# One weight gradient by Strassen-Winograd: five plain pairs first, three resident sums, D folded into C and 7, eight additions on GpSimd

## The chip, the cores and the metric

The kernel runs on one core of one Trainium2 chip. The metric is the device time of one execution in microseconds (us); three runs of the kernel before gave 162.25, 162.35 and 162.43, median 162.35. One more execution was profiled; the lines of the profile come from that one.

## What is computed

```python
def setup_inputs():
    batch, m, k, n = 16, 512, 1024, 768
    ...
def reference(input, grad_output):            # (16, 512, 1024) and (16, 512, 768), float32
    grad_weight = np.einsum('bmk,bmn->kn', input, grad_output)
    return grad_weight.astype(np.float32)     # (1024, 768)
```

It is one matrix product: the 8192 rows of `input` (1024 columns, X in the kernel) against the 8192 rows of `grad_output` (768 columns, G), summed over the rows. The kernel rounds both to bf16 on the way in and sums in f32.

## The kernel before, in words

**Tiles.** The rows are read in 32 pairs of 256. A pair has an x tile and a g tile, bf16, loaded by DMAs that POOL issues and that convert from f32 (lines 152 and 153; up to `PAIRS_HELD` = 14 pairs are held). Only the very first pieces come as f32 over two other queues (`xf`, `gf`) and are rounded by VectorE and ScalarE (`round_by`).

**Four quarters.** The output is cut in four quarters: A (first 512 of k, left 384 of n), B (first, right), C (second, left), D (second, right). Each quarter has four blocks, q = 0 to 3, of 128 x 384, and a block fits in one of the eight PSUM banks.

**Two ways to add a pair.** `LOADS` says how each pair is multiplied. A plain pair ("s") is two steps of 128 rows, each 16 matmuls (four quarters, four blocks): 32 a pair. A Strassen pair ("P") takes seven products instead of eight: 28 matmuls of 128x384. Its products go to seven sums, each with four blocks: 1 and A (from x and g as they are), B and C (one operand raw, one a sum) and 5, 6 and 7 (both operands sums). The sums of x and of g are made on VectorE in six steps, `x0 x1 x2` (`sum_x`, lines 183 to 187) and `g0 g1 g2` (`sum_g`, lines 193 to 197). At the end the sums are combined: A + 1; 6 + 1; 7 + 6; then from 5 one gets 5 - 6 and 5 - 7; B + (5 - 6), C + 7, D + (5 - 7), where D holds the plain pairs' share alone. `SHARED` names for each sum the one that is added to it.

**32 sums, 8 banks.** There are 28 running sums of Strassen products and four of D, and eight banks. A's four blocks keep a bank each until they are complete (banks 7, 3, 4 and 1); the others take turns in banks 0, 2, 5 and 6. A block that leaves its bank is kept in SBUF (`acc` or `macc`), in one of three ways:

- `c`: ScalarE copies the bank out (`close`, line 327), for a bank that already held the whole sum;
- `v`: VectorE copies it (line 329) or adds it to what SBUF holds (line 331), and in the end adds the shared sum too (lines 307 to 312) and starts the store to DRAM, on SP's queue (ScalarE's for the last 128 columns);
- before that, `f` (`fill`, line 274) may let ScalarE copy the SBUF sum back into a bank, so that the matmuls go on adding to it.

**The order is written out by hand.** `PLAN` is one list of tokens, and each engine runs its own instructions strictly in the order of that list: `A1.2` is two matmuls on block A1, `53@6.2` opens bank 6 for block 3 of product 5 and does two matmuls, `c53`, `v53`, `f53@0` are as above, `x1.12` is a step of the sums of pair 12, `r2` a rounding. An instruction that has to wait holds up all that stands behind it on its engine. The lines: matmuls 287, fills 274, copies out 327, warm-up matmuls 135 (`WARMUP`: on constants, before the first data come).

Of the kernel before, what the change touches and what calls it, by code (L numbers as in the profile page):

```python
# [9 lines left out]
P = 128  # L10

LOADS = "ssssssPPPPPPPPPPPPPPPPPPPPPPPPPs"

PLAN = (
    "A0@7.1 A3@3.1 A1@4.1 C3@5.1 C2@0.1 C1@2.1 r0 cC3 C0@6.1 vC2 A2@1.1 cC1 D0@5.1 vC0 B0@0.1 cD0 D1@2.1 "
    "r1 r3 B3@6.1 r2 D3@5.2 vB0 r4 A1.1 A2.1 cD1 vB3 A3.1 B1@0.2 cD3 B2@2.2 vB1 D2@6.2 cB2 C0@5.1 C1@0.1 "
    "vD2 A0.1 fD0@2 A2.1 vC0 A3.1 fD1@6 A1.1 D0.2 vC1 C2@5.2 cD0 D1.2 vC2 C3@0.2 cD1 B0@2.2 vC3 B3@5.3 "
    "fB1@6 vB0 A0.2 fB2@0 vB3 B1.2 fC0@2 B2.2 cB1 C1@5.2 vB2 C0.2 fD2@6 A3.1 vC1 D3@0.2 cC0 D2.2 fC2@5 "
    "vD3 C3@2.1 A1.1 cD2 A2.1 vC3 C2.1 B0@0.1 D1@6.1 vC2 D0@2.1 vB0 fD2@5 A3.2 vD1 A1.2 fB0@0 D2.2 vD0 "
    "B1@6.2 cD2 B0.2 vB1 B2@2.2 cB0 B3@5.2 vB2 C0@6.2 fC1@0 A2.2 vB3 fC2@2 C1.2 vC0 C3@5.2 cC1 C2.2 vC3 "
    "fD0@6 A0.2 D1@0.4 vC2 D3@5.4 vD1 D0.4 vD3 C3@2.2 vD0 B3@5.2 C0@0.2 vC3 fC1@6 A3.2 vB3 fB2@2 A0.2 vC0 "
    "C1.2 fD2@5 B2.2 cC1 D2.2 vB2 C2@0.2 cD2 B0@6.2 vC2 fB1@2 A1.4 vB0 fC1@0 B1.4 C2@5.2 cB1 D2@6.2 vC2 "  # L30
    "C1.2 fD0@2 A2.4 vD2 fD3@5 vC1 fC3@6 D0.2 D3.2 vD0 C3.2 cD3 C0@0.2 vC3 B2@2.4 vC0 fB3@6 B0@5.4 vB2 "
    "fD1@0 B3.4 fC0@2 vB0 A3.1 g0.6 fB1@5 A3.3 vB3 A0.2 g1.6 A0.2 fC1@6 D1.1 g2.6 D1.3 A2.2 vD1 A1.3 x0.6 "
    "fC2@0 C0.3 C1.1 x1.6 C1.2 cC0 C2.1 x2.6 C2.2 cC1 C3@2.1 g0.7 C3.2 cC2 B1.3 fD0@6 vC3 D2@0.2 g1.7 cB1 "
    "D0.2 vD2 fD3@2 A2.1 A3.1 A0.1 g2.7 cD0 10@5.1 D3.2 c10 x0.7 11@0.2 cD3 12@6.2 v11 13@5.2 c12 50@2.1 "
    "x1.7 50.1 c13 51@0.2 x2.7 52@6.2 c50 g0.8 53@5.2 c51 70@2.2 v52 c53 A2.1 g1.8 A3.1 fB3@0 72@6.2 v70 "
    "73@5.2 c72 g2.8 B3.2 v73 63@2.2 cB3 B2@6.1 x0.8 B2.1 fC1@5 A1.2 v63 A0.2 71@0.1 x1.8 71.2 vB2 62@2.3 "
    "c71 x2.8 C1.2 c62 g0.9 60@6.3 cC1 61@2.1 g1.9 61.2 fB0@0 v60 10@5.2 c61 g2.9 B0.3 v10 fC3@6 C2@2.2 "
    "cB0 x0.9 C2.1 C3.3 fC0@5 vC2 A2.2 f52@0 C0.1 x1.9 cC3 C0.2 A3.1 x2.9 A3.1 cC0 12@2.1 g0.10 12.1 52.2 "
    "f63@5 v12 B1@6.3 c52 g1.10 63.2 f13@2 vB1 11@0.2 c63 A0.1 g2.10 13.2 v11 72@5.2 c13 x0.10 A1.2 f51@0 "
    "53@6.2 v72 A0.1 f70@2 A3.1 51.1 x1.10 f50@5 51.2 v53 70.3 c51 x2.10 50.2 f73@6 g0.11 50.1 B3@0.3 c70 "  # L40
    "v50 73.2 fB2@2 g1.11 73.1 vB3 A2.1 f10@5 B2.2 c73 g2.11 B2.1 10.1 x0.11 10.2 cB2 C1@0.3 c10 x1.11 "
    "62@6.2 f71@2 vC1 A3.1 A1.1 f61@5 A0.1 x2.11 71.2 f60@0 g0.12 71.1 61.3 v62 c71 60.1 g1.12 60.2 c61 "
    "B0@2.1 g2.12 fB1@6 B0.2 v60 11@5.2 vB0 B1.2 fC0@0 A2.1 x0.12 A2.1 cB1 A0.1 C0.3 fC2@2 v11 A3.1 fC3@6 "
    "A1.1 x1.12 C2.3 cC0 x2.12 13@5.2 f53@0 g0.13 13.1 C3.3 cC2 v13 53.2 f52@2 g1.13 53.1 vC3 12@5.3 c53 "
    "g2.13 52.3 f72@6 v12 63@0.2 x0.13 c52 63.1 72.3 f62@5 v63 A2.1 f51@2 A1.1 x1.13 62.2 c72 51.1 x2.13 "
    "51.2 f50@0 v62 73@6.3 c51 g0.14 50.3 f70@5 v73 A3.1 fB2@2 A0.1 70.1 g1.14 c50 70.2 g2.14 B3@6.3 c70 "
    "B2.1 x0.14 B2.2 10@5.3 vB3 cB2 C1@0.1 x1.14 C1.2 f60@6 v10 11@2.3 x2.14 60.2 f61@5 g0.15 60.1 A1.1 "
    "61.3 c60 vC1 A0.1 g1.15 71@6.3 c61 v11 B0@0.1 fB1@5 g2.15 B0.2 v71 A2.2 fC2@2 A3.1 x0.15 A3.1 f52@6 "
    "B1.3 vB0 C2.2 cB1 x1.15 C2.1 52.2 cC2 x2.15 52.1 C0@0.1 fC3@5 g0.16 C0.2 A1.1 c52 A0.1 vC0 C3.3 "
    "f12@2 g1.16 13@6.3 vC3 12.2 g2.16 f62@5 12.1 v13 53@0.3 c12 x0.16 62.3 f72@6 A1.1 v53 63@2.3 c62 "  # L50
    "x1.16 f50@0 72.4 v63 f51@5 50.1 g0.17 50.2 c72 70@2.1 x2.16 70.2 c50 g1.17 51.3 v70 73@6.2 g2.17 c51 "
    "73.1 B2@0.1 x0.17 fB3@2 B2.2 A2.2 fC1@5 v73 B3.3 x1.17 C1.3 vB2 cB3 10@6.2 x2.17 cC1 10.1 71@0.1 "
    "g0.18 f11@2 71.2 A3.2 v10 f60@5 11.1 g1.18 11.2 v71 60.3 c11 g2.18 61@6.3 c60 x0.18 A0.3 fC0@2 v61 "
    "B1@0.3 fB0@5 x1.18 C0.3 fC2@6 vB1 B0.2 cC0 x2.18 B0.1 C2.1 g0.19 f12@0 C2.2 C3@2.3 cB0 vC2 12.2 "
    "f62@5 g1.19 12.1 vC3 A1.2 c12 53@6.1 g2.19 53.2 f52@2 x0.19 13@0.4 v53 A3.2 52.1 x1.19 f72@6 52.3 "
    "v13 62.2 x2.19 c52 62.2 g0.20 73@0.3 c62 g1.20 63@2.4 f51@5 v73 72.1 g2.20 72.2 fC1@0 v63 51.3 c72 "
    "x0.20 A2.3 c51 70@2.1 x1.20 70.3 f71@5 x2.20 50@6.4 v70 C1.1 g0.21 C1.2 fB2@2 A0.2 v50 cC1 B2.2 "
    "g1.21 B2.2 fB3@6 g2.21 A1.2 cB2 B3.4 x0.21 71.3 cB3 B0@0.2 x1.21 c71 B0.1 10@6.2 x2.21 10.2 vB0 "
    "C2@2.2 g0.22 C2.1 f61@0 A3.2 vC2 11@5.3 g1.22 11.1 f60@2 61.4 v10 g2.22 60.4 v11 c61 x0.22 C0@6.4 "
    "f53@0 c60 12@5.1 x1.22 12.3 vC0 B1@2.2 x2.22 B1.2 g0.23 C3@6.4 v12 53.2 g1.23 53.2 vB1 A1.2 c53 vC3 "  # L60
    "52@5.3 f73@2 g2.23 13@0.2 x0.23 13.2 A2.3 v52 A0.1 x1.23 A0.2 f51@5 v13 A3.2 51.1 x2.23 51.2 g0.24 "
    "51.1 73.3 c51 g1.24 73.1 C1@6.1 g2.24 C1.2 c73 63@5.4 vC1 f72@2 70@0.1 x0.24 f71@6 70.2 72.5 v63 v70 "
    "f62@5 A1.2 x1.24 c72 71.2 g0.25 71.2 f50@0 62.1 x2.24 fB2@2 62.2 g1.25 62.2 c71 B2.1 g2.25 B2.3 c62 "
    "50.4 vB2 B0@6.1 x0.25 f10@2 B0.3 c50 C2@5.1 x1.25 C2.3 f11@0 vB0 10.2 x2.25 10.2 g0.26 11.4 c10 vC2 "
    "B3@6.2 f60@2 g1.26 B3.2 c11 g2.26 B3.1 60.4 vB3 fB1@0 61@5.2 fC0@6 x0.26 61.2 c60 B1.4 v61 12@2.1 "
    "x1.26 fC3@5 12.3 vB1 C0.2 g0.27 f53@0 C0.2 x2.26 C3.2 cC0 g1.27 C3.2 v12 53.3 cC3 g2.27 53.1 52@6.4 "
    "v53 A2.1 x0.27 f51@0 A2.3 v52 A3.3 x1.27 A3.1 f70@6 A0.2 x2.27 A0.2 g0.28 A1.3 13@2.1 g1.28 13.2 "
    "g2.28 13.1 C1@5.4 v13 51.4 f73@2 vC1 70.1 x0.28 f63@5 70.3 c51 73.1 x1.28 73.3 c70 x2.28 73.1 63.2 "
    "c73 g0.29 63.3 f72@2 50@0.1 g1.29 50.2 c63 g2.29 50.1 71@6.4 v50 f62@5 72.4 fB0@0 v71 62.1 x0.29 "
    "f11@6 62.3 c72 B0.1 x1.29 B0.3 c62 x2.29 11.4 fB2@2 vB0 fC2@5 B2.1 g0.30 B2.4 f10@0 v11 C2.4 vB2 "  # L70
    "f11@6 10.1 g1.30 f12@2 10.3 vC2 A2.1 g2.30 A2.2 c10 x0.30 12.4 f13@5 f10@0 x1.30 11.1 13.3 c12 v11 "
    "10.1 A3.1 f61@2 x2.30 A3.2 v13 f62@6 A1.3 v10 f63@5 61.5 f60@0 62.2 v61 60.5 v62 f71@2 A2.2 f72@6 "
    "v60 A3.2 A1.2 vA2 f70@0 A0.5 vA3 vA1 70.3 vA0 63.2 v70 f50@1 71.2 72.2 fC0@3 v63 50.2 f73@0 v71 C0.6 "
    "f51@4 v72 fC1@5 v50 51.3 f52@2 fC2@7 C1.5 vC0 fD0@6 v51 fB0@1 52.4 fD1@3 B0.4 vC1 fB1@4 C2.3 v52 "
    "fD2@5 B1.7 vB0 fB2@2 vC2 73.2 vB1 B2.3 v73 f53@1 D0.2 D1.2 fC3@4 vB2 53.4 vD0 C3.6 vD1 v53 fD3@0 "
    "fB3@2+7 D2.2 D3.2 vC3 B3.7 vD2 vD3 vB3 "
).split()


WARMUP = [("b", 512), ("f", 512), ("f", 512), ("b", 512)]  # L80
PAIRS_HELD = 14
SUMS_HELD = 10

MERGED = 2


@with_exitstack
def kernel(
# [162 lines left out]


    SHARED = {"A": "1", "B": "5", "C": "7", "D": "1", "6": "1", "7": "6"}

    done = {(p, q): 0 for p in streams for q in range(Q)}
    fresh = {(p, q): True for p in streams for q in range(Q)}
    closed = set()
    opened = {}
    used = {7}
    stores = [0]  # L260

    def bank(b):
        return psum.tile([P, 512], f32, name=f"bank{b}")

    def fill(p, q, b, b2):
        assert (p, q) not in opened and not fresh[p, q] and b in used
        src = sum_of(p, q)
        if b2 is None:
            parts = [(bank(b), 0, NH)]
        else:  # L270
            assert b2 in used
            parts = [(bank(b), 0, 256), (bank(b2), 256, NH)]
        for tile_, c0, c1 in parts:
            nc.scalar.copy(out=tile_[:, 0 : c1 - c0], in_=src[:, c0:c1])  # L274
        opened[p, q] = (parts, True)

    def multiply(p, q, b, n):
        first = (p, q) not in opened
        if first:
            opened[p, q] = ([(bank(b), 0, NH)], False)  # L280
            used.add(b)
        parts, carried = opened[p, q]
        for tile_, c0, c1 in parts:
            for j in range(n):
                at = done[p, q] + j
                stat, mov = operands(p, streams[p][at], q)
                nc.tensor.matmul(  # L287
                    tile_[:, 0 : c1 - c0],
                    stat,
# [7 lines left out]
    def close(engine, p, q):  # L297
# [34 lines left out]
        if final:  # L332
            closed.add((p, q))
# [51 lines left out]
```

## Time and profile before

| | |
|---|---|
| median of three runs | 162.35 us |
| the profiled execution | 162.31 us, of which the span in the profile is 160.5 us |
| granted TensorE clock, mean | 1.00 |
| loads | 58.72 MB read from DRAM |
| fills on ScalarE (line 274) | 71 + 70 instructions, some 0.48 us each |
| copies out on ScalarE (line 327) | 61 + 45 instructions, some 0.48 us each |
| adds on VectorE (line 331) | 54 + 41 instructions, some 0.55 us each |
| sums of x and g on VectorE | 25 times six instructions, 0.35 to 0.68 us each |
| instructions of POOL | DMA issues (0.53 us each) and memsets (0.10) |

How to read it. The busy table gives the time in which an engine works on at least one instruction; instructions of one engine overlap, so the distance from one start to the next in a queue that never waits (its step) is shorter than the duration that the page prints. The slices cut the span in 40 parts and give each engine's share in tenths. The chain that ended last follows the end of the span backwards, at each step to whatever released the instruction. The timeline lists merged runs: start, length, engine, line, what is written and read, and how many instructions (x4). A wait is put down to whatever came last.

### The profile page before, as it was taken

To read this page: it belongs to the slowest core of one execution; us is meant where nothing else is said; L and a number is where in the kernel's file an instruction comes from. 1 tells how busy PE (TensorE), PEld (TensorE's weight loads), DVE (VectorE), ACT (ScalarE), POOL (GpSimd) and SP (SyncE) were. 2 spreads that over 40 slices of the span, in tenths; PEclk is the share of its full clock that TensorE was granted. 3 is DMA by queue.
4 is the path that set the end of the run, shared out by engine and by line. 5 is a ranking of instruction groups with operands and counts; after the bars stand their busy time and mean duration, and the time that the engine had idled before them with its cause. 6 is when DMAs were issued, how large, how long until landed. Compare 5 with 4: busy or idle time off the path is not lost.

```text
span 160.5 us, 2776 instructions
## 1 busy us (share of the span) xinstructions
PE 155.3 (97%) x937; PEld 91.9 (57%) x937; DVE 142.7 (89%) x323; ACT 112.8 (70%) x253; POOL 34.8 (22%) x69
## 2 busy tenths in 40 slices
PE   8899999999999999999999999999999999999990
PEld 3355556556556656655655655665665665556560
DVE  0788986989999999999989998998899998989992
ACT  3779737749888999968777786534777368877730
POOL 7452222122221222222122222212222100000000
PEclk9999999999999999999999999999999999999999
DMA  5999999999999999999999999999999999924385
GB/s 176 295 213 213 210 216 213 213 213 212 213 212 212 213 213 214 210 214 213 215 214 213 213 212 212 213 212 214 213 210 213 215 212 214 212 43 157 137 294 196
DMA packets 12830, 33.40 MB, mean 208 GB/s; under 512 B 1424, under 2 KB 4624, under 8 KB 12816
## 3 DMA queue, kind: packets, MB, share of 16 engines
q0 software_dynamic: 9360, 28.64, 90.2%
q1 hardware_dynamic: 3024, 3.47, 6.3%
q10 hardware_dynamic: 432, 1.11, 1.8%
q8 instruction: 7, 0.11, 0.3%
q14 instruction: 7, 0.06, 0.1%
HBM read 58.72 MB, written 3.15 MB: 385 GB/s over the span
## 4 chain that ended last, share of the span: by engine, by line
DMA 48%; PE 44%; DVE 2%; issue 2%; POOL 1%; DVEq 0%; POOLq 0%
DMA xp<-in_input_dram 48%; PE bank L287 44%; POOL gp L157 1%; DVE acc L312 1%; DVE xe L183 0%; POOL xp L159 0%; DVE acc L331 0%; DVE macc L331 0%; DVEq L380 0%; DVE xe L185 0%; POOLq L153 0%; POOLq L369 0%; POOLq L152 0%
## 5 line engine op out<-in xcount | busy, mean ns | idle before, releaser
L287 PE MATMUL bank<-gp,xp 128*128 128x384 bf16 (+2 forms) x631 | 109.8, 324 | 0.6 <-DVE xp L201 0.6
L287 PEld LDWEIGHTS <-xp 128*128 128x128 bf16 x631 | 61.1, 98 | 42.5 <-DVE xp L201 1.3
L287 PE MATMUL bank<-ge,xe 128*128 128x384 bf16 x300 | 56.2, 326 | 0.1
L274 ACT COPY bank<-macc 128x384 f32<-128x384 f32 x71 | 33.6, 484 | 13.2 <-DVE macc L331 5.6
L287 PEld LDWEIGHTS <-xe 128*128 128x128 bf16 x300 | 29.3, 98 | 19.9 <-issue 0.6
L274 ACT COPY bank<-acc 128x384 f32<-128x384 f32 (+1 forms) x70 | 32.3, 479 | 9.1 <-DVE acc L329 5.5
L327 ACT COPY macc<-bank 128x384 f32<-128x384 f32 x61 | 28.6, 479 | 9.5 <-PE bank L287 8.1
L331 DVE TENSOR_TENSOR acc<-bank,acc 128x384 f32<-128x384 f32 x54 | 28.7, 552 | 2.8 <-PE bank L287 1.2
L153 POOL DMA_DIRECT2D xp<-in_input_dram x30 | 16.0, 532 | 53.3 <-DMA xp<-in_input_dram 28.0
L327 ACT COPY acc<-bank 128x384 f32<-128x384 f32 x45 | 21.4, 480 | 6.5 <-PE bank L287 6.0
L152 POOL DMA_DIRECT2D gp<-in_grad_output_dram x30 | 16.0, 533 | 37.1 <-DMA gp<-in_grad_output_dram 15.0
L331 DVE TENSOR_TENSOR macc<-bank,macc 128x384 f32<-128x384 f32 x41 | 22.5, 551 | 0.5 <-PE bank L287 0.2
L183 DVE TENSOR_TENSOR xe<-xp 128x1024 bf16<-128x1024 bf16 x25 | 17.1, 683 | 1.2 <-DMA xp<-in_input_dram 1.2
L329 DVE COPY acc<-bank 128x384 f32<-128x384 f32 x24 | 13.1, 553 | 3.0 <-PE bank L287 2.4
L193 DVE TENSOR_TENSOR ge<-gp 128x768 bf16<-128x768 bf16 x25 | 13.8, 550 | 0.0
L187 DVE TENSOR_TENSOR xp<-xp,xe 128x512 bf16<-128x512 bf16 x25 | 10.5, 419 | 0.4
L185 DVE TENSOR_TENSOR xe<-xe,xp 128x512 bf16<-128x512 bf16 x25 | 10.5, 418 | 0.3
L197 DVE TENSOR_TENSOR gp<-ge,gp 128x384 bf16<-128x384 bf16 x25 | 8.8, 352 | 0.3
L195 DVE TENSOR_TENSOR ge<-gp,ge 128x384 bf16<-128x384 bf16 x25 | 8.7, 350 | 0.2
L312 DVE TENSOR_TENSOR acc<-bank,macc 128x384 f32<-128x384 f32 (+2 forms) x17 | 8.0, 522 | 0.0
L329 DVE COPY macc<-bank 128x384 f32<-128x384 f32 x14 | 7.6, 552 | 0.4 <-PE bank L287 0.4
L201 DVE CAST gp<-gf 128x192 bf16<-128x192 f32 (+1 forms) x2 | 0.7, 360 | 4.9 <-DMA gf<-in_grad_output_dram 4.9
(17 smaller groups left out, 21.6 us busy)
## 6 DMA issues: line engine op xcount, KB each, us to landing
xp<-in_input_dram POOLq DMA_DIRECT2D x30, 512.0 KB, 16.9
gp<-in_grad_output_dram POOLq DMA_DIRECT2D x30, 384.0 KB, 16.7
out_dram<-acc SPq DMA_DIRECT2D x12, 192.0 KB, 1.9
xf<-in_input_dram ACTq DMA_DIRECT2D x2, 512.0 KB, 5.0
gp<-in_grad_output_dram POOLq DMA_DIRECT2D x3, 192.0 KB, 6.6
out_dram<-acc SPq DMA_DIRECT2D x6, 96.0 KB, 1.7
xp<-in_input_dram POOLq DMA_DIRECT2D x2, 256.0 KB, 8.0
gf<-in_grad_output_dram SPq DMA_DIRECT2D x2, 192.0 KB, 4.2
```

What stands on the lines that cost most here:

```text
L152: nc.gpsimd.dma_start(out=gp, in_=G[rows, :].rearrange("(p m) n -> p m n", m=2))
L153: nc.gpsimd.dma_start(out=xp, in_=X[rows, :].rearrange("(p m) k -> p m k", m=2))
L183: nc.vector.tensor_sub(out=xe[:, 0:2, :], in0=x[:, 1::-1, :], in1=x[:, 3::-2, :])
L185: nc.vector.tensor_sub(out=xe[:, 2, :], in0=xe[:, 0, :], in1=x[:, 0, :])
L187: nc.vector.tensor_add(out=x[:, 1, :], in0=x[:, 2, :], in1=xe[:, 2, :])
L193: nc.vector.tensor_add(out=ge[:, 0:2, :], in0=g[:, 0:2, :], in1=g[:, 1::2, :])
L274: nc.scalar.copy(out=tile_[:, 0 : c1 - c0], in_=src[:, c0:c1])
L287: nc.tensor.matmul(tile_[:, 0 : c1 - c0], stat, mov[:, c0:c1], start=first and j == 0, stop=True, skip_group_check=True,)
L312: nc.vector.tensor_add(out=dst[:, c0:c1], in0=b, in1=sum_of(SHARED[p], q)[:, c0:c1])
L327: nc.scalar.copy(out=dst, in_=b)
L329: nc.vector.tensor_copy(out=dst, in_=b)
L331: nc.vector.tensor_add(out=dst, in0=b, in1=dst)
```

## The change

- **Loads.** `LOADS` has five plain pairs and then 27 Strassen pairs; before, six plain ones, 25 Strassen ones and a plain one at the end.
- **Banks.** A0, A1 and A2 keep a whole bank each (`@R`: banks 5, 6 and 7) until they are complete; A3 takes turns with all the others in banks 0 to 4. Groups in a bank become shorter.
- **D.** When D's plain share is complete, it is added to C and subtracted from 7 at an eviction that these blocks have anyway (`k`, on VectorE: 8 of them). D's own result is then 5 - 7, made in the step that closes 5, and D has no late fill and eviction any more.
- **GpSimd.** Eight additions of sums in SBUF go to POOL (`add_shared`): for A0 to A3, C0 and C3 it adds the shared sum after ScalarE has copied the bank out and then stores (`q`); for blocks 60 and 72 it adds the shared sum ahead of the last eviction (`p`).
- **Warm-up.** One bf16 matmul of 512 columns and 32 of 128 instead of two f32 and two bf16 ones of 512.
- **Stores.** The first four stores are halved instead of the first three.
- **Order.** `PLAN` is new from its first token to its last. Its beginning and its end are shown.

```diff
-LOADS = "ssssssPPPPPPPPPPPPPPPPPPPPPPPPPs"
+LOADS = "sssssPPPPPPPPPPPPPPPPPPPPPPPPPPP"
...
-    "A0@7.1 A3@3.1 A1@4.1 C3@5.1 C2@0.1 C1@2.1 r0 cC3 C0@6.1 vC2 A2@1.1 cC1 D0@5.1 vC0 B0@0.1 cD0 D1@2.1 "
+    "A0@R.1 C0@0.1 C2@1.1 cC0 C1@2.1 r0 C3@3.1 vC2 A3@4.1 cC1 B3@0.1 A2@R.1 cC3 vA3 A1@R.1 D1@1.1 D2@2.1 r3 r1 "
...
-    "f51@4 v72 fC1@5 v50 51.3 f52@2 fC2@7 C1.5 vC0 fD0@6 v51 fB0@1 52.4 fD1@3 B0.4 vC1 fB1@4 C2.3 v52 "
-    "fD2@5 B1.7 vB0 fB2@2 vC2 73.2 vB1 B2.3 v73 f53@1 D0.2 D1.2 fC3@4 vB2 53.4 vD0 C3.6 vD1 v53 fD3@0 "
-    "fB3@2+7 D2.2 D3.2 vC3 B3.7 vD2 vD3 vB3 "
+    "A0.1 63@0.1 x2.28 60@3.2 v71 60.1 63.2 v12 63.1 B2@2.2 g0.29 53@4.3 vB2 53.1 B0@1.1 g1.28 B0.1 f51@2 B0.1 "
+    "v53 60.2 A1.1 v63 A1.1 f62@4 A1.2 g2.28 A1.1 62.1 vB0 62.2 x0.29 62.2 52@0.2 c62 g0.30 52.3 x1.29 f50@4 "
+    "52.1 51.1 v60 51.2 50.1 v52 50.1 c51 50.1 13@1.1 g1.30 13.1 c50 g1.29 13.2 x0.30 f73@2 13.2 72@0.1 f70@3 "
+    "72.1 v13 72.1 f63@4 72.1 70.1 x1.30 70.1 f10@1 70.1 g2.30 70.2 v72 73.2 x2.29 73.2 A0.1 g2.29 A0.1 g0.31 "
+    "12@0.2 A1.1 x2.30 63.2 g1.31 63.1 10.1 g2.31 10.2 x0.31 10.2 12.1 A0.1 c10 A2.1 x1.31 A2.1 cA0 A2.1 v12 "
+    "p60 A1.1 f11@1 63.1 13@5.1 x2.31 70.1 cA1 60@0.1 v13 60.1 cA2 60.1 73.1 11.1 f62@6 v60 11.1 qA2 11.1 "
+    "f50@7 11.1 v63 11.1 62.1 fC3@5 62.1 v70 62.1 qA0 f53@0 50.2 v62 C3.1 fC0@3 C3.2 v50 c11 C3.1 p72 72@6.2 "
+    "f61@4 53.2 f52@1 53.1 v73 C0.1 qA1 C0.1 fA3@7 v72 C0.2 cC3 52.1 v53 52.1 A3.1 fB2@2 qC3 A3.2 fB0@6 A3.1 "
+    "61.1 v52 61.1 cC0 61.2 f71@0 B2.1 qC0 B2.1 cA3 B2.1 v61 71.2 f51@1 71.1 vB2 B0.1 qA3 fC1@4 B0.2 v71 51.1 "
+    "fB1@5 51.1 vB0 C1.1 fB3@2 C1.2 v51 C1.1 fC2@3+7 B1.4 B3.1 vC1 B3.3 vB1 B3.1 C2.2 vB3 C2.4 vC2 "
...
-WARMUP = [("b", 512), ("f", 512), ("f", 512), ("b", 512)]
+WARMUP = [("b", 512)] + 32 * [("b", 128)]
+HALVED = 4
+ASIDES = 0
+RESIDENT = 3
+FOLDED = True
...
-    SHARED = {"A": "1", "B": "5", "C": "7", "D": "1", "6": "1", "7": "6"}
+    SHARED = {"A": "1", "B": "5", "C": "7", "D": "6", "6": "1", "7": "6"}
...
+    def resident_parts(q):
+        if RESIDENT < 4:
+            return [(bank(8 - RESIDENT + q), 0, 0, NH)]
...
+    def store(p, q, c0, c1, engine):
+        row = q if p in "AB" else Q + q
+        at = 0 if p in "AC" else NH
+        cuts = [c0, (c0 + c1) // 2, c1] if stores[0] < HALVED else [c0, c1]
+        stores[0] += 1
+        for d0, d1 in zip(cuts, cuts[1:]):
+            engine.dma_start(out=OUT[:, row, at + d0 : at + d1], in_=sum_of(p, q)[:, d0:d1])
+
...
+    def multiply(p, q, where, n):
+        first = bool(where)
+        if where == "R":
+            opened[p, q].append((resident_parts(q), True))
...
+        for tile_, at, c0, c1 in parts:
+            b = tile_[:, at : at + c1 - c0]
+            to = dst[:, c0:c1]
+            if engine == "c":
+                assert carried or away
+                assert not final or p in "ABC"
+                nc.scalar.copy(out=to, in_=b)
+            elif engine == "k":
+                assert carried and not final and last("D", q) and not opened["D", q]
+                d = sum_of("D", q)[:, c0:c1]
+                (nc.vector.tensor_add if p == "C" else nc.vector.tensor_sub)(out=to, in0=b, in1=d)
+                folded.add((p, q))
+            elif final and p == "5":
+                assert carried and {("6", q), ("7", q)} <= closed
+                nc.vector.tensor_sub(out=to, in0=b, in1=sum_of("6", q)[:, c0:c1])
+                d = sum_of("D" if FOLDED else "6", q)[:, c0:c1]
+                nc.vector.tensor_sub(out=d, in0=b, in1=sum_of("7", q)[:, c0:c1])
+                if FOLDED:
+                    store("D", q, c0, c1, queue)
+            elif final and (p, q) not in prepared:
+                assert carried and (SHARED[p], q) in closed and (p != "D" or ("5", q) in closed)
+                nc.vector.tensor_add(out=to, in0=b, in1=sum_of(SHARED[p], q)[:, c0:c1])
+                if p in "BCD" and len(parts) == 2:
+                    store(p, q, c0, c1, nc.sync if c0 == 0 else nc.scalar)
+            elif carried:
+                assert (p, q) not in prepared
+                nc.vector.tensor_copy(out=to, in_=b)
+            else:
+                nc.vector.tensor_add(out=to, in0=b, in1=to)
+        if final and p in "ABCD" and engine == "v" and (len(parts) == 1 or p == "A"):
+            store(p, q, 0, NH, queue)
+        if last(p, q) and not opened[p, q] and not (engine == "c" and p in "ABC"):
+            closed.add((p, q))
+        spilled.add((p, q))
+
+    def add_shared(p, q, prepare, queue):
+        assert (SHARED[p], q) in closed
+        dst = sum_of(p, q)
+        nc.gpsimd.tensor_add(out=dst, in0=dst, in1=sum_of(SHARED[p], q))
+        if prepare:
+            assert all(not carried for _, carried in opened[p, q]) and len(opened[p, q]) < 2
+            prepared.add((p, q))
         else:
+            assert last(p, q) and not opened[p, q] and (p, q) not in closed
+            store(p, q, 0, NH, queue)
```

## The prediction, made before the changed kernel ran

> **What bounds the kernel now.** I read the busy table and the slices first, then the chain that ended last, the timeline, and the waits.
>
> ```profile
> PE 155.3 (97%) x937; PEld 91.9 (57%) x937; DVE 142.7 (89%) x323; ACT 112.8 (70%) x253; POOL 34.8 (22%) x69
> ...
> DMA  5999999999999999999999999999999999924385
> GB/s 176 295 213 213 210 216 213 213 213 212 213 212 212 213 213 214 210 214 213 215 214 213 213 212 212 213 212 214 213 210 213 215 212 214 212 43 157 137 294 196
> ```
>
> Two resources are full to the end of the loads: TensorE, and the DMA engines, at a steady 213 GB/s until slice 35 (about 142 us). The chain tells how they meet:
>
> ```profile
> 12.32 17.40 DMA xp<-in_input_dram
> ...
> 30.00 17.07 DMA xp<-in_input_dram
> ...
> 47.70 16.63 DMA xp<-in_input_dram
> ...
> 64.61 17.76 DMA xp<-in_input_dram
> ...
> 84.41 70.98 PE bank L287 x435
> ```
>
> Issue plus time to landing gives the x tiles of pairs 5, 9, 13 and 17 at 29.72, 47.07, 64.33 and 82.37, so a pair comes every 4.3 to 4.5 us; the trace's landing of the last, pair 31, is 142.71. From 84.41 the chain stays on TensorE: 435 matmuls in 70.98 us. The timeline gives the paces:
>
> ```profile
> 84.89 0.98 PE L287 MATMUL bank<-gp,xp 128*128 128x384 bf16 x5
> ...
> 147.87 1.71 ACT L274 COPY bank<-acc 128x384 f32<-128x384 f32 x4
> ```
>
> ```profile
> 50.15 0.47 ACT L327 COPY macc<-bank 128x384 f32<-128x384 f32 x1
> 50.52 0.49 ACT L274 COPY bank<-macc 128x384 f32<-128x384 f32 x1
> ```
>
> ```profile
> 145.63 1.94 DVE L312 TENSOR_TENSOR macc<-bank,macc 128x384 f32<-128x384 f32 x4
> ```
>
> Five matmuls occupy 0.98 us and one alone takes 0.326 (the page's mean for this shape), so their starts stand (0.98 - 0.326)/4 = 0.1635 apart; over all 902 undisturbed steps of the trace it is 0.1625. A fill's step is (1.71 - 0.48)/3 = 0.41, a copy-out's 50.52 - 50.15 = 0.37, an eviction's on VectorE (1.94 - 0.545)/3 = 0.465. These steps, not the longer durations, fill a queue; the same reading gives 0.60, 0.33 and 0.33 for the three sums of x and 0.465, 0.27 and 0.27 for those of g, 2.26 per Strassen pair.
>
> TensorE's first real matmul starts at 5.19 and its last ends at 156.86. Of these 151.67 us, 924 matmuls (the seven split ones counted once) take 924 x 0.1625 = 150.15, the last one's drain 0.16, and all gaps together 1.36. I call the lag of a matmul behind a stream without gaps its **slip**: 1.36 at the end. What makes it:
>
> ```profile
> DVE xe L183 <- DMA xp<-in_input_dram: 1.2, 3, 0.5
> ```
>
> Pair 17 lands at 82.37, where a stream without gaps would use it at 81.6 and VectorE would add it at 81.1; TensorE stands for 0.3 us just behind. So the kernel is bound by its matmuls, held back by the loads.
>
> **The change, part by part.** The sum goes against the profiled run's own 162.31 (span 160.5 and 1.8 around it); the median of the three runs is 162.35.
>
> *Matmuls.* Before: 7 plain pairs of 32 and 25 Strassen pairs of 28, 924. After: 5 x 32 + 27 x 28 = 916. 8 x 0.1625 = **-1.30 us**, on the path. Seven split matmuls become six: nothing.
>
> *Loads.* Their order and sizes do not change from pair 2 on, and a buffer's last matmul stands 26 us or more before the issue that needs it, so the landings stay. Laid against the landings of before, the new order uses pairs sooner: pair 17 first at 81.1 (landing 82.37: slip at least 1.28), pair 22 at 102.2 (103.51: 1.30), pair 31 at 141.5 (142.71: 1.17). A matmul follows its landing by about 0.05 (16.31 to 16.36 for pair 2), and the sums queued on VectorE behind a landing ask for up to 1.44 (pair 21). So the loads alone ask for a slip of about 1.4, as now. What TensorE loses early, up to that, costs nothing: the loads take it anyway.
>
> *Copies and evictions.* Evictions on VectorE fall from 166 to 152 (-14 x 0.465 = -6.5), and two more pairs add 2 x 2.26 = 4.5: 2 us less, off the path. D folded into C and 7 changes 8 copies to adds, both 0.55 in their rows, and drops D's four late fills and evictions. Four banks rotated beside A's four; now five rotate and A3 among them, in shorter groups, so ScalarE gets 135 copies out (from 106) and 173 fills (from 141). In the first 614 matmuls (99.8 us) it had 86 x 0.372 + 87 x 0.413 + two roundings = 68.5 us of steps; now 110 x 0.372 + 135 x 0.413 + 0.6 = **97.3 us**. TensorE hides that only while the steps stay at their shortest. I followed the stretches between a group's last matmul, its copy (at the soonest 0.36 later), what is queued behind, and the matmul that needs the fill (0.53 after the fill starts). The worst: the first group of C0 ends 0.16 us into the stream; 0.36, then 14 copies, 9 fills and 2 roundings (9.54), then 0.53 make 10.60, and the matmul stands at 10.24: 0.36 late. From 91.3 a copy of 73, 4 further copies and 8 fills (5.16) stand ahead of C3's fill: 6.06 where 5.85 us are to be had, 0.21 late. Others through VectorE come within 0.1. The first lies in what the loads take; the second comes on top of their 1.4: slip 1.6, **+0.25**. Bounds for all queue waits: 0 (everything within the loads' slip) to 2.5 (10 ns on each of 245 copies).
>
> *GpSimd's eight additions* (128x384, f32) have no row. On POOL the rows are a memset of one column, 0.10, and a DMA issue, 0.53; VectorE's add of the shape takes 0.55. I take 0.55 to 1.1 and keep 0.10 and 2.2, four times VectorE, as ends. They are queued behind the last load's issue (125.62 + 0.53), and so is a library reload that the new order has there; POOL is then free until the copy of 10 lands at about 142.4, 16 us of cover. The first, for 6, may last 1.4 us until the eviction it serves; the fourth, for 7, is queued behind two of A's. Following them, matmuls stay on time up to 1.4 us an addition, lose 0.13 at 1.5 and 1.13 at 2.0. Forecast 0. The last, of A3, is released near 150.5 and stored by 154. The Trainium skill speaks against it: "GPSIMD Engine Reference", section 3.1, has this kind of add of 2048 columns at 4497 ns, twice VectorE; 384 columns would by estimate take 0.84, and the sum would still be the same.
>
> *Warm-up and start.* The first 512-column bf16 matmul of the warm-up took 0.586, its last, the same shape, 0.380: 0.206 more, about what 512 columns take at the steady pace (0.1625 x 512/384 = 0.217), so it began at half pace; the f32 passes (1061 ns, the last 701) put the change near 3.9 us. The new warm-up streams 512 + 32 x 128 = 4608 columns, at half pace 4608 x 2 x 0.1625/384 = 3.9 us, from 0.78 to 4.7 if none of it were faster; the first data are rounded at about 5. The second real matmul now is C0's, whose columns VectorE rounds third (until about 5.4), and B3 needs the right half of g (0.36 from 6.03) in seventh place: some 0.4 us, which takes the place of the 0.45 that the start loses now and lies in the loads' slip. Forecast 0.
>
> *End.* From the last matmul's end the span runs 160.5 - 156.86 = 3.6 us: eviction, issue, store. The new end has the same shape (a 256 and a 128 column part on two queues): 0.
>
> Sum: 162.31 - 1.30 + 0.25 = **161.3**.
>
> **Rivals.**
> *ScalarE's queue becomes the bound* (slower). Place: the first 100 us. TensorE gives it 99.8 + the 1.4 of slip = 101.2 us for 97.3: 3.9 us over 245 copies, 16 ns each. Beyond, every 10 ns cost 2.45 us; at 26 ns, time is 162.31 - 1.30 + 2.45 = 163.5. For: its usual step is longer than the shortest (half of the fills stand 0.465 or more apart). Against: those are mostly waits with room; eight fills in a row ran at 0.414 (146.2 to 149.1). 0.13.
> *Small waits in crossings of ScalarE and VectorE eat the gain* (the change removes matmuls and yet saves nothing): 0.7 to 1.6 us more than the sums, 162.0 to 162.6, say 162.3. For: many stretches have under 0.1 to spare. Against: the same sums give 0.7 for before, all within its 1.36. 0.13.
> *GpSimd at 2 us*: 161.3 + 1.1 = 162.4. For: no row. 0.06.
> *Cold start.* If small matmuls do not open the clock, the first 3.4 us of real ones run at half pace: 10 matmuls lost, 1.7, plus the 0.45 that the start loses to the roundings now; the loads' 1.4 hide most of the 2.15: 161.3 + 0.7 = 162.0. The skill's "TensorE: Matmul & The Clock Gate", Part 1, has this window free-running, so its phase may shift; the trace has one sample. 0.05.
> The forecast (161.0 to 161.7): 0.63.
>
> **How the numbers follow.** A measurement of this kernel tells about 0.2% (0.32 us) from no change. Faster (under 162.03): the forecast, half of the cold start, and a third of the crossings, 0.63 + 0.03 + 0.04 = 0.70. Slower (over 162.67): ScalarE 0.13 and a little of GpSimd, 0.15. Same: the rest, 0.15. Range 160.9 to 162.5: below, the loads' floor less 0.2 (no queue wait at all and the spread of runs); above, crossings and GpSimd at 2 us; ScalarE as the bound is left out.
>
> **What would show it.** The loads' landings as before, pair 31 at 142.7; the last matmul's end near 155.8; ScalarE's slices at 9 up to slice 25 with its steps near 0.37 and 0.41; VectorE's waits for loads at pairs 17 to 22; POOL's additions under 1.4 us. Wrong, if TensorE waits long for fills in the first 100 us, if the additions take 2 us, or if the first real matmuls start later than 5.3.

## The result, and the profile after

| | before | after |
|---|---|---|
| median | 162.30 us (162.23 to 162.43, 4 runs) | 163.44 us (163.17 to 163.71, 4 runs) |
| profiled execution | 162.31, span 160.54 | 163.17, span 161.36 |
| first real matmul | 5.19 | 5.36 |
| last matmul's end | 156.86 | 156.46 |
| from there to the end of the span | 3.68 | 4.90 |

The ratio is 1.0069, 95% interval 1.0055 to 1.0084: slower, where 161.3 and faster was forecast. TensorE does finish sooner, by 0.40 us instead of 1.05. What comes behind it is 1.22 us longer, and that was forecast at nothing.

The busy table and some slices of the kernel after:

```profile
PE 154.7 (96%) x955; PEld 93.1 (58%) x955; DVE 143.6 (89%) x321; ACT 128.3 (80%) x314; POOL 42.6 (26%) x77
...
ACT  3799998999999999999999998996543323839920
...
GB/s 164 294 212 213 215 215 213 212 212 214 210 212 212 214 216 210 213 212 216 216 209 215 211 213 216 210 215 212 212 212 211 215 214 212 203 24 70 148 368 195
```

ScalarE went from 112.8 to 128.3 us and is nearly full from the third slice to the 27th (8 to 109 us). The loads keep their 213 GB/s; pair 22's x lands at 103.82 (before 103.52) and pair 31's at 142.87 (before 142.71). What is new is at the right end: in slice 39 (153 to 157 us) the core moves 368 GB/s, and these are the stores. In before the same bytes began to leave at 144.35 and the last slices read 157 137 294 196; now the first store is issued at 147.15. Windows of 3 us show it closer. The columns are length, busy time of PE, PEld, DVE, ACT and POOL (with instructions), clock, DMA share, GB/s. Before:

```profile
147.00:150.00 3.00, 3.00 (x20) 1.79 (x19) 3.00 (x8) 2.65 (x8) 0.00 (x0) 1.00 0.52 178
150.00:153.00 3.00, 3.00 (x21) 1.82 (x19) 3.00 (x7) 2.11 (x5) 0.00 (x0) 1.00 0.44 157
153.00:156.00 3.00, 3.00 (x22) 1.92 (x21) 3.00 (x8) 1.22 (x4) 0.00 (x0) 1.00 0.93 338
156.00:159.00 3.00, 0.86 (x12) 0.65 (x9) 1.39 (x4) 0.00 (x0) 0.00 (x0) 1.00 0.78 268
```

After:

```profile
147.00:150.00 3.00, 3.00 (x20) 1.75 (x18) 3.00 (x8) 2.91 (x8) 2.82 (x4) 1.00 0.41 131
150.00:153.00 3.00, 3.00 (x20) 1.76 (x18) 3.00 (x8) 3.00 (x9) 2.68 (x4) 1.00 0.41 131
153.00:156.00 3.00, 3.00 (x24) 2.00 (x22) 3.00 (x7) 1.37 (x5) 0.50 (x1) 1.00 1.02 362
156.00:159.00 3.00, 0.46 (x7) 0.27 (x4) 0.76 (x3) 0.00 (x0) 0.00 (x0) 1.00 1.03 360
```

Before has some idle share left in every window. After stores at 131 GB/s while there is room and is then at the DMA engines' limit for six microseconds, two and a half of them after TensorE is done at 156.46. In that limit a 192 KB store lands every 0.53 us (196,608 bytes in 0.53 us are 371 GB/s). The halves of 96 KB come earlier, while the DMA engines are about half busy (0.53 from 150.6 to 152.8 us), and still land only every 0.48 us; yet one of their packets takes 36 ns where one of a whole store takes 67 (medians). So the bytes are not what spaces the halves; what does is not shown. The line of stores decides the end, not the last store.

Why it starts late is in the timeline of POOL in the kernel after (start, length, engine, line, operation, written<-read, count, and in brackets the idle time before):

```profile
146.12 1.96 POOL L392 TENSOR_TENSOR acc<-acc,macc 128x384 f32<-128x384 f32 x2 [0.55 <-ACT acc L360]
148.26 1.00 POOL L392 TENSOR_TENSOR macc<-macc 128x384 f32<-128x384 f32 x1 [0.18 <-DVE macc L375]
149.22 2.11 POOL L392 TENSOR_TENSOR acc<-acc,macc 128x384 f32<-128x384 f32 x2
```

These are A2 and A0, block 72, and A1 and C3. An addition takes 1.00 us; A1's ends at 150.22. And VectorE, in the same execution:

```profile
148.57 0.54 DVE L370 TENSOR_TENSOR acc<-bank,macc 128x384 f32<-128x384 f32 x1
```

That is D0, ready at 149.11. `PLAN` fixes the order of TensorE, VectorE, ScalarE and POOL, but not that of SP, which issues the stores. There the scheduler put A1's first half ahead of D0's two halves (and, later, C3 ahead of D3, C0 ahead of D2 and A3 ahead of B2, where nothing had to wait any more). SP issued nothing from 148.94 until A1 was ready, A1's first half at 150.25, and only then D0's, which had been ready for over a microsecond. Its waits for POOL's additions, in the view of waits (in total, times, longest):

```profile
SPq L295 <- POOL acc L392: 146.8, 2, 145.5
```

The longer of the two is the wait for the first store of all; the other, about 1.3 us, is this one. From 150.25 on SP issued one store every 0.49 us without a pause until 157.93. The data of the last block, C2, were ready at 156.97; the last landing was at 160.02.

Of the 1.22 us, each part rounded, 0.51 lie between the last matmul's end and the last issue (0.56, now 1.07), 0.35 between that and the last landing (2.14, now 2.49), and 0.37 after it (0.97, now 1.34). In the last part SP waits for the landings' semaphores (the counters that tell it that a store has landed) one by one, some 0.06 each; in after the one that lands last stands first among eight, in before second to last.

The main other loss is in the stream of matmuls, in the chain of the kernel after, 97 to 105 us (start, length, what):

```profile
97.46 0.48 ACT macc L360
97.94 0.80 ACT bank L313 x2
...
103.18 1.22 ACT bank L313 x3
104.39 0.04 issue
104.43 0.65 PE bank L335 x3
```

From 97.46 on the chain runs through ScalarE's copies and fills and comes back to TensorE only at 104.43: C3's fill is late, TensorE stands for 0.24 us just before. It is the stretch that the prediction had 0.21 late.

### The profile page after: what moved, and what is told of

Read it like the earlier page. It is cut to its first block, busy times and chain, and to the rows that moved or that the text cites. A ratio compares the mean times of both kernels' runs of the same rounds, so it can differ in the third digit from the quotient of the medians.

```text
span 161.4 us, 2881 instructions
## 1 busy us (share of the span) xinstructions
PE 154.7 (96%) x955; PEld 93.1 (58%) x955; DVE 143.6 (89%) x321; ACT 128.3 (80%) x314; POOL 42.6 (26%) x77
## 4 chain that ended last, share of the span: by engine, by line
PE 83%; ACT 10%; DMA 3%; issue 1%; DVE 0%; DVEq 0%; ACTq 0%
PE bank L335 83%; ACT bank L313 5%; ACT acc L360 3%; DMA xf<-in_input_dram 3%; ACT macc L360 1%; DVEq L448 0%; DVE xp L206 0%; DVE acc L375 0%; ACTq L360 0%; DVEq L375 0%
## 5 line engine op out<-in xcount | busy, mean ns | idle before, releaser
L335 PE MATMUL bank<-gp,xp 128*128 128x384 bf16 (+1 forms) x598 | 107.8, 325 | 0.9 <-DVE xp L206 0.6
L335 PEld LDWEIGHTS <-xp 128*128 128x128 bf16 x598 | 57.9, 98 | 40.8 <-DVE xp L206 1.4
L335 PE MATMUL bank<-ge,xe 128*128 128x384 bf16 x324 | 62.6, 326 | 0.0
L313 ACT COPY bank<-macc 128x384 f32<-128x384 f32 x84 | 40.7, 511 | 7.5 <-DVE acc L382 4.2
L313 ACT COPY bank<-acc 128x384 f32<-128x384 f32 (+1 forms) x89 | 42.1, 506 | 4.7 <-DVE macc L382 3.9
L360 ACT COPY macc<-bank 128x384 f32<-128x384 f32 x70 | 33.4, 511 | 7.6 <-PE bank L335 7.4
L360 ACT COPY acc<-bank 128x384 f32<-128x384 f32 x65 | 31.4, 499 | 2.9 <-PE bank L335 2.7
L382 DVE TENSOR_TENSOR acc<-bank,acc 128x384 f32<-128x384 f32 x42 | 22.4, 554 | 1.2 <-PE bank L335 0.9
L382 DVE TENSOR_TENSOR macc<-bank,macc 128x384 f32<-128x384 f32 x36 | 19.4, 552 | 0.4 <-PE bank L335 0.3
L392 POOL TENSOR_TENSOR acc<-acc,macc 128x384 f32<-128x384 f32 x6 | 5.9, 1001 | 0.9 <-ACT acc L360 0.7
```

What stands on the lines that cost most here:

```text
L313: nc.scalar.copy(out=tile_[:, at : at + c1 - c0], in_=src[:, c0:c1])
L335: nc.tensor.matmul(tile_[:, at : at + c1 - c0], stat, mov[:, c0:c1], start=fresh, stop=True, skip_group_check=True,)
L360: nc.scalar.copy(out=to, in_=b)
L382: nc.vector.tensor_add(out=to, in0=b, in1=to)
```

## The experiments

Theory at the start: the stores at the end (their number, their order on SP, the wait for GpSimd) cost about 1.2, ScalarE's fills some tenths. Rivals: the halves cost nothing and the end is only moved; GpSimd is the wrong engine; the warm-up. All ratios are to the kernel before on the same chip, with 95% intervals; its medians there were 162.26 to 162.38. Differences from after are differences of medians; after's four runs lie between 163.17 and 163.71. Where nothing else is said, the edit is made in the kernel after.

**No halves.**

```diff
-HALVED = 4
+HALVED = 0
```

> The first four stores are left whole, so SP issues four stores fewer; nothing else changes. Theory T (the end is set by SP's queue of stores: in the changed kernel SP issues one store every 0.49 us without a pause from 150.25 to 157.93, and the last leaves 0.6 us after its data are ready): two of the halves stand in that stretch, so the queue should catch up with VectorE, the last issue move from 1.07 to about 0.6 us behind the last matmul, and the time fall by 0.4 to 0.9 us, to 162.5 to 163.0. Rival (the tail is set by the landing of the bytes, 21 stores of 3.15 MB in 10 us): the same bytes, so less than 0.2 us either way, 163.3 to 163.6. Theory S (ScalarE's queue) and theory W (warm-up) expect no change.

162.37 us (161.98 to 162.72, 12 runs), ratio 1.0005 [0.9995, 1.0016]: 1.07 less than after. The tail behind the last matmul shrinks from 4.90 to 4.06; the last landing is at 159.47 instead of 160.02, with four stores fewer in the line. Two of the four halved blocks, A1 and D0, stood in the stretch in which SP issued without a pause: their four halves took it from 150.25 to 152.12, 1.87 us, where whole stores follow each other every 0.49. With whole stores the same window reads 214 GB/s instead of 131:

```profile
150.00:153.00 3.00, 3.00 (x20) 1.74 (x19) 3.00 (x8) 3.00 (x8) 2.69 (x4) 1.00 0.60 214
```

The last issue is then 0.54 behind the last matmul instead of 1.07, as theory T had it. Of the 0.84 that the tail lost, 0.53 are this, 0.12 lie between the last issue and the last landing, and 0.19 behind it, where the last landing's semaphore now stands fourth of eight.

**The same halves in the kernel before** (eight blocks halved instead of three).

```diff
-                    cut = (c0 + c1) // 2 if stores[0] < 3 else c1
+                    cut = (c0 + c1) // 2 if stores[0] < 8 else c1
```

> The kernel before, with its first eight stores halved and not its first three: five stores more, none of them among the last eight. Theory T2 (a halved store costs the end only where stores stand in a backlog: a half takes its 0.48 us of the stores' path as a whole one takes 0.53; in the kernel before, the early stores come every 0.9 to 1.4 us and leave room): the time stays within 0.2 us of before. Rival (each store has its price at the end, by its issue or by one more semaphore): 5 x 0.2 to 0.5, 1.0 to 2.5 us slower.

162.40 (162.15 to 162.79, 12), ratio 1.0004 [0.9993, 1.0014]. Where the line has idle room, five halves more cost nothing. The price belongs to a line without pauses and not to a half as such.

**SP in the order of `PLAN`.** D0's stores now go before A1's, and D3's, D2's and B2's before those of C3, C0 and A3; no instruction is added or removed.

```diff
-    ctx.enter_context(tc.manual_schedule(engines={E.PE, E.DVE, E.Activation, E.Pool}))
+    ctx.enter_context(tc.manual_schedule(engines={E.PE, E.DVE, E.Activation, E.Pool, E.SP}))
```

> The changed kernel with the stores on SP in the order of the list of tokens, so that D0's two halves stand ahead of A1's (in the changed kernel they wait behind A1's first half, that is for GpSimd's addition, while SP stands from 148.94 to 150.25 though D0 is ready at 149.1). Theory T2 (the end is the backlog of stores, each 0.5 us, that starts at 150.25): the backlog starts about 1 us sooner, and the last landing comes 0.5 to 1.0 us sooner, until the data of C2 (ready at 157.0) set it: 162.4 to 162.9. Rival (the semaphores or the teardown make the end): no change, 163.3 to 163.6.

162.12 (161.74 to 163.47, 12), ratio 0.9996 [0.9975, 1.0016]: 1.3 less than after, by the order alone. The tail is 3.74 instead of 4.90. The SP timelines, after and then this experiment:

```profile
147.15 10.78 SPq L295 DMA_DIRECT2D out_dram<-acc  x20
```

```profile
148.54 9.97 SPq L295 DMA_DIRECT2D out_dram<-acc  x20
```

The same twenty issues take 0.8 less from the first to the last. (In this execution the whole stream of matmuls ran some 1.4 us late, for a reason that comes below with the warm-up; so lengths are compared here, not times. It is one of two long ones of the twelve, 163.36 and 163.47; the other ten lie between 161.74 and 162.34.)

**A second queue for the last stores.** ScalarE, idle by then, issues those of C1 and B3.

```diff
-... vC1 B3.3 vB1 B3.1 C2.2 vB3 C2.4 vC2 "
+... vC1a B3.3 vB1 B3.1 C2.2 vB3a C2.4 vC2 "
```

> Two of the last stores, of C1 and of B3, are issued by ScalarE, whose copies are over by then, and not by SP; nothing else changes. Theory T: SP is free for the last part of C2 as soon as its data are ready; the last issue comes about 0.6 us behind the last matmul, 0.5 sooner, and the semaphores at the end are waited for in another order: 0.4 to 0.9 us faster, 162.5 to 163.0. Rival (landing of the bytes): under 0.2 us either way, 163.3 to 163.6.

162.82 (162.64 to 164.47, 12), ratio 1.0051 [1.0025, 1.0076]; three of the twelve, 164.28 to 164.47, are long ones, and the ratio has them in it. The time falls by 0.62, as theory T forecast, but not for its reason. SP's last issue moves from 157.53 to 156.81, 0.72 sooner, and the last landing only from 160.02 to 159.93. This execution's window:

```profile
156.00:159.00 3.00, 0.38 (x6) 0.20 (x3) 0.68 (x3) 0.00 (x0) 0.00 (x0) 0.97 1.03 362
```

The DMA engines are as full as in after. So my theory in its first form, that SP cannot issue fast enough, fell for the last three microseconds: there the bytes are in the way, not the issues. The Trainium skill has the rule in "DMA: Bandwidth & Descriptors", section "Issuing engines are not separate DMA queues": issuing from several engines saves only time on the sequencer. The 0.72 and the 0.09 agree. The profiled execution is 0.40 shorter than after's; 0.28 of that lie behind the last landing (1.34, now 1.06), where the semaphores are waited for in another order.

**The additions on VectorE.**

```diff
-        nc.gpsimd.tensor_add(out=dst, in0=dst, in1=sum_of(SHARED[p], q))
+        nc.vector.tensor_add(out=dst, in0=dst, in1=sum_of(SHARED[p], q))
```

> The eight additions of GpSimd are made by VectorE instead, at the same places of the list; nothing else changes. Theory G (GpSimd's additions, 1.0 us each and one after the other, are what starts the stores late and what costs the last 0.2 us of slip): the stores start about 1 us sooner and the time falls by 0.3 to 1.0 us, to 162.4 to 163.1. Rival (VectorE is full in the last 12 us, 9 of 10 tenths, so eight more steps of 0.25 to 0.47 us hold up evictions and TensorE): the last matmul ends 0.5 to 3 us later, and the time is 163.9 to 166.

165.77 (164.82 to 166.73, 4), ratio 1.0214 [1.0170, 1.0258]. These four fall in two pairs, 164.82 and 165.09, and 166.45 and 166.73. The last is the profiled one, and it has the slow start that comes below with the warm-up: its matmuls stand 0.32 apart until 9.64 us, and its slip at the 610th matmul is 3.53 where after has 1.90. That 1.6 is not the additions' price; the first pair, taken as free of it, is 1.5 longer than after. A window of this experiment, then of after:

```profile
150.00:155.00 5.00, 3.84 (x23) 2.24 (x23) 5.00 (x12) 4.29 (x11) 0.00 (x0) 1.00 0.43 138
```

```profile
150.00:155.00 5.00, 5.00 (x33) 2.95 (x31) 5.00 (x12) 4.37 (x12) 3.18 (x4) 1.00 0.65 223
```

VectorE is full (5.00 of 5) either way, and with the additions on it TensorE does 23 matmuls instead of 33. From the 850th matmul to the 900th its slip grows by 2.6, in after by 0.15; that difference does not hang on the start. GpSimd is the better engine for them; what hurts is where their results stand in the line of stores.

**ScalarE's price.** The first 110 copies out of sums that have been in SBUF before copy 192 of 384 columns; the rest of these sums is left out.

```diff
-                nc.scalar.copy(out=to, in_=b)
+                copies[0] += 1
+                cut = 192 if (p, q) in spilled and copies[0] <= 110 else c1 - c0
+                nc.scalar.copy(out=to[:, 0:cut], in_=b[:, 0:cut])
```

> Of the first 110 copies out on ScalarE, those of sums that SBUF already holds copy 192 of 384 columns (the other half of such a sum keeps an older value: the output is not the product). That takes some 0.15 us from each of about 90 steps, 14 us of ScalarE's work. Theory S (half of the missing gain is ScalarE's queue: gaps of TensorE at 16.0, 24, 33.6 and 104.0 us, 1.1 us together, behind chains of copies and fills): these gaps go, the slip at matmul 600 falls from 1.9 to about 1.4, where the loads hold it, and the last matmul ends 0.4 to 0.7 us sooner, the time with it: 162.7 to 163.0. Rival (the gaps are the loads' own): they stay, and the time changes by less than 0.2 us.

162.74 (162.58 to 162.98, 10), ratio 1.0026 [1.0017, 1.0034]. The slip, counted in each run from its own first matmul, falls at the 500th from 1.66 to 1.13, at the 610th only from 1.90 to 1.59; the last matmul ends 0.39 sooner, at 156.07. The tail stays at 4.90: the two losses add. Between the 500th and 610th something else took over, in this experiment's timeline:

```profile
103.86 0.82 PE L335 MATMUL bank<-gp,xp 128*128 128x384 bf16 x4 [0.19 <-DMA xp<-in_input_dram]
```

TensorE now waits for pair 22's load.

**The loads' floor.** As above, and half of g of pairs 8, 12 and 16 is set to zero instead of loaded (192 KB each in bf16).

```diff
-            nc.gpsimd.dma_start(out=gp, in_=G[rows, :].rearrange("(p m) n -> p m n", m=2))
+            pairs_of_g = G[rows, :].rearrange("(p m) n -> p m n", m=2)
+            if u in (8, 12, 16):
+                nc.gpsimd.dma_start(out=gp[:, 0, :], in_=pairs_of_g[:, 0, :])
+                nc.gpsimd.memset(gp[:, 1, :], 0.0)
+            else:
+                nc.gpsimd.dma_start(out=gp, in_=pairs_of_g)
```

> The kernel with the short copies (ScalarE copies out half of the columns of sums that SBUF holds already: those sums keep older values), and besides half of g of pairs 8, 12 and 16 is not loaded but set to zero: 0.59 MB less of the first loads, the landings from pair 16 on some 2.8 us sooner. Theory L (with ScalarE light, the loads hold TensorE: the gap of 0.36 us before pair 22's first matmul): that gap goes, the slip at matmul 610 falls from 1.59 to 1.1 to 1.2, the last matmul ends 0.4 sooner, near 155.7, and the time falls by 0.3 to 0.5 us from the short copies' 162.74. Rival (the gap is a wait on ScalarE or VectorE that stays): no change, 162.6 to 162.9.

162.25 (162.09 to 163.76, 10), ratio 1.0007 [0.9987, 1.0028]. The slip at the 610th matmul is 1.08, where halved copies alone had 1.59, and the last matmul ends at 155.57. One of the ten, 163.76, is a long one of the kind told below. In the same place TensorE now runs through:

```profile
102.41 1.79 PE L340 MATMUL bank<-gp,xp 128*128 128x384 bf16 x10
```

So the loads do ask for a slip, and at this place that is what was left when ScalarE was relieved.

**The warm-up of before.**

```diff
-WARMUP = [("b", 512)] + 32 * [("b", 128)]
+WARMUP = [("b", 512), ("f", 512), ("f", 512), ("b", 512)]
```

> The warm-up matmuls of before (two bf16 and two f32 of 512 columns) in the changed kernel. Theory W (the small warm-up matmuls cost at the start: first real matmul at 5.36 instead of 5.19, first f32 piece landed at 5.05 instead of 4.77): the first real matmul comes back to 5.2, and the time falls by 0.1 to 0.3 us. Rival (the start differs from run to run, and the loads swallow it anyway): the time stays within 0.2 us of 163.4, whatever the first matmul does.

163.06 (162.86 to 163.50, 6), ratio 1.0046 [1.0030, 1.0062]. The first real matmul is at 5.21 instead of 5.36, the last ends at 156.35 instead of 156.46, and the span is 0.11 shorter. A steady price of the small warm-up would be 0.1 to 0.4; the intervals of this ratio and after's overlap, so it is not shown.

**The new warm-up in the kernel before** (the same edit the other way).

> The kernel before with the small warm-up and nothing else of the change. Theory C: most executions within 0.2 us of before; one or two in twelve longer, by what is left of 10 matmuls lost (1.7 us) once the loads' slip of 1.2 has taken its part: 0.5 to 1.5 us. Theory W: all executions 0.1 to 0.4 us slower than before.

162.39 (162.26 to 164.10, 11), ratio 1.0019 [0.9999, 1.0039]. Ten runs lie with those of before; one took 164.10. Such long executions, 1.3 to 1.8 us over their neighbours, came in 9 of 81 of the kernels with the 33 small matmuls (two of them with the additions on VectorE) and in none of about a hundred with the old four. Two were profiled, those of the store-order experiment and of the additions on VectorE; that the other seven are of the same kind is argued from their length. The first's TensorE timeline, then that of after:

```profile
0.78 4.00 PE L140 MATMUL bank<-const-bfloat16-1.0 128*128 128x512 bf16 x33 [0.78 <-PEq L437]
5.32 6.95 PE L335 MATMUL bank<-gp,xp 128*128 128x384 bf16 x29 [0.54 <-DVE xp L206]
```

```profile
0.78 4.00 PE L140 MATMUL bank<-const-bfloat16-1.0 128*128 128x512 bf16 x33 [0.78 <-PEq L437]
5.36 6.86 PE L335 MATMUL bank<-gp,xp 128*128 128x384 bf16 x38 [0.58 <-DVE xp L206]
```

The warm-up is the same to 10 ns, yet nine matmuls fewer follow in the same time: in the first, matmuls stand 0.32 apart until 9.3 us and 0.1625 from then on, in the second only the first matmul is long (0.50 us, the next 0.34). The record of the granted clock in the two traces begins, at full clock, at 9.36 and at 5.84 us. (The views print a clock of 1.00 for the time ahead of it too, so the steps have to be read.) In the other twelve traces it begins between 3.93 and 5.93, save for that of the additions on VectorE, where it begins at 9.78. The two beginnings are 3.52 apart, about one window of 3.41 that the Trainium skill gives in "TensorE: Matmul & The Clock Gate", Part 1, with windows running free of the kernel's start. By that page the same warm-up can open the clock at one window's end or miss it until the next; the traces agree.

**Together: no halves, SP in order, the old warm-up.** The edits are the three above.

> The changed kernel with three things put right: no store halved, the stores on SP in the order of the list, the warm-up of before. Theory T2: from the 1.07 us that the unhalved stores gave, another 0.3 to 0.6 by the order of the stores, and 0.1 by the start: the end is set by C2's data again (3.7 us from the last matmul to the end, as before), the last matmul ends near 156.4, so the span is 160.1 and the time 161.7 to 162.1, less than both kernels. Rival (the gains are the same gain twice: once the backlog is gone nothing is left): 162.2 to 162.5.

161.56 (161.33 to 161.78, 6), ratio 0.9955 [0.9941, 0.9969]: faster than both kernels. The first matmul is at 5.03, the last ends at 156.04, and the tail is 3.52. Its windows:

```profile
150.00:153.00 3.00, 3.00 (x20) 1.74 (x19) 3.00 (x8) 3.00 (x9) 2.80 (x3) 1.00 0.76 270
153.00:156.00 3.00, 3.00 (x25) 2.02 (x23) 2.79 (x7) 0.95 (x4) 0.08 (x1) 1.00 1.04 368
156.00:159.00 3.00, 0.04 (x1) 0.00 (x0) 0.54 (x2) 0.00 (x0) 0.00 (x0) 0.98 0.67 227
```

The stores now use the room from 150 to 153 (270 GB/s where after has 131), and in the last window the DMA engines are two thirds busy instead of all. The single savings (1.07, 1.32 and 0.38) add to 2.77, and together they bring 1.88: halves and order shorten the same line and overlap, for each alone already brings the last issue to 0.54 behind the last matmul, as here. The eight additions are still on GpSimd, and yet the tail is shorter than before's 3.68: as such they cost the end nothing.

**Together, with the small warm-up.** The same without the warm-up's edit.

> The repaired kernel (no halved store, stores in the order of the list) with the small warm-up matmuls of the changed kernel, one of 512 columns and 32 of 128. Theory C (the small warm-up now and then fails to open the clock before the first real matmuls: in one profiled execution twelve of them ran 0.325 us apart until 9.4 us, and 7 of 54 executions with the small warm-up were 1.3 to 1.7 us longer than their neighbours, none of 75 with the old one): most executions within 0.2 us of 161.6, one or two in twelve near 163. Theory W (it costs in every execution): all executions 0.2 to 0.4 us above 161.6.

161.74 (161.40 to 161.86, 6), ratio 0.9966 [0.9954, 0.9978]. No execution is near 163, and the median is 0.14 above the old warm-up's; neither theory is shown by six.

**Together, with nine wide bf16 matmuls as the warm-up.**

```diff
-WARMUP = [("b", 512)] + 32 * [("b", 128)]
+WARMUP = 9 * [("b", 512)]
```

> The repaired kernel with a warm-up of nine bf16 matmuls of 512 columns: as many columns as the small warm-up (4608), in big matmuls, as long (4.0 us at half pace). Theory C1 (it is the length and the pause before the first real matmul that count): now and then an execution near 163, as with the small ones. Theory C2 (it is the kind: 33 small matmuls with 33 weight loads keep the array less busy than few big ones): none of twelve near 163, all at 161.3 to 161.8.

161.69 (161.28 to 161.75, 5), ratio 0.9963 [0.9950, 0.9976]. The three warm-ups lie within 0.2 us and their intervals overlap: nothing between them is settled by these runs, and five or six are too few to see a miss that comes in one of nine.

## Why the prediction was wrong, step by step

- *Matmuls, -1.30*: right. The step is still 0.1624, so the stream without gaps is 1.30 shorter.
- *Loads, a slip of about 1.4*: right in kind, some 0.25 too small. The landings did not stay: pair 22's x, which the prediction had at 103.51, came at 103.82, pair 31's 0.16 later than before. The experiments on copies and loads show the floor: with the copies relieved the slip at the 610th matmul stayed at 1.59 from the run's own start, 1.66 from 5.19, until some loads were dropped.
- *Copies, +0.25*: right mechanism and place (C3's fill, 0.21 forecast, 0.24 measured), size too small. Counted from 5.19 the slip at the end is 2.26, not 1.6; halving the copies gives back 0.39 of it. Behind the 800th matmul another 0.19 is lost (0.15 in before), which no experiment took apart.
- *GpSimd's additions, 0*: right for the matmuls. They take 1.00 us, inside 0.55 to 1.1, and nearer to the 0.84 estimated from the Trainium skill ("GPSIMD Engine Reference", section 3.1) than to VectorE's 0.55.
- *Warm-up and start, 0*: nearly. The first matmul is 0.17 later, at 5.36, past the 5.3 that the prediction named as a sign of being wrong; and the cold start that had a chance of 0.05 occurs, in 9 of 81 executions as far as their length tells, and costs 1.3 to 1.8 us there.
- *End, "the new end has the same shape ...: 0"*: this step failed. I compared the last store of the two kernels and they are alike. I did not lay out the twenty stores ahead of it, as I had done for every copy of ScalarE: when each block is ready, which store SP has next, how long each takes. The one store that the prediction followed, A3's, "stored by 154", was issued at 154.08 and landed at 156.20. Measured: +1.22 in the profile, and the experiments on order and halves take back 1.16 and 0.84 of it, each alone, and 1.38 together. With the end so mended the kernel takes 161.56, near the forecast.

In the profiled run: 162.31 - 1.30 + 0.25 = 161.26, and 161.26 + 0.17 (start) + 0.48 (slip) + 1.22 (end) = 163.13; the rest to 163.17 lies outside the span of the profile. None of the rivals was the one that came. ScalarE as the bound was priced at 163.5, almost the measured time, but its sign is missing: relieved of half the work of 110 copies, the kernel gains 0.4 to 0.7, not 2.2.

Left open: the 0.37 behind the last landing, of which 0.19 to 0.28 went away in the experiments on the stores, was never changed by itself; what spaces the halves 0.48 apart; the steady price of the small warm-up; and whether it misses for its small matmuls or for its length. That completions bunch because work went to GpSimd is argued from the start of the stores (144.35, now 147.15) and was not tried by moving single additions.

## What to carry to other kernels

A saving on the busiest engine is worth what is left of it at the last landing: list every store with the time at which its data are ready, its place on the issuing queue, its step there and its time at the full DMA rate, and see whether the line still ends with the last block. A queue whose order nobody wrote can put a store that waits ahead of stores that are ready; here that alone took 1.16 us of the tail, nearly all that the removed matmuls gave. Here halved stores were free only where the line had idle time.

## What the runs showed of the hardware

- A 192 KB store (128 rows of 1536 bytes) lands every 0.53 us when the DMA engines are full (share 1.02). A 96 KB half issued 0.39 us behind another lands 0.48 us behind it, at a share of about half: half the bytes, nine tenths of the time, though its packets take 36 ns instead of 67.
- GpSimd adds 128x384 f32 in 1.00 us (0.96 from start to start), VectorE in 0.54 (0.465).
- ScalarE's copies kept their shortest steps (medians 0.371 out, 0.413 in over the first 105 us) at a busy share of 80%, without the loss of 10 to 26 ns each that a rival had.
